# The gates of an encoder layer by Strassen's scheme, with their work placed among the attention heads

## The chip, the core and the metric

The kernel runs on one core of one Trainium2 chip. The core has TensorE (PE in the profile), which multiplies matrices out of the on-chip memory SBUF into the accumulator PSUM, VectorE (DVE), ScalarE (ACT) and GpSimd (POOL), which work on tensors elementwise, and queues that start DMA transfers: most are started by SyncE (SP), some by ACT. Each engine takes its own instructions in a fixed order and waits for the others by semaphores. The metric is the device time of one execution in microseconds (us); smaller is better.

## The reference

One residual layer over x, 1024 tokens by 1024 channels, all float32.

```python
h = rmsnorm(x, g_mix)
z = h @ w_in                     # 1024 x (512 pooling | 1024 q | 1024 k | 1024 v)
y_pool = pool_mixer(u_pool, w_pool_grp, pool_scale)
y_attn = diff_attention(q, k, v, ...)            # 8 heads, two softmax maps each
gates  = sigmoid(h @ w_gate + b_gate)            # 1024 x 2048
merged = gates[..., :D] * (y_pool @ w_branch_pool) + gates[..., D:] * (y_attn @ w_branch_attn)
x = x + merged @ w_out
h2 = rmsnorm(x, g_ffn)
x = x + square(relu(h2 @ w_up)) @ w_down         # 4096 hidden channels
```

The change is about one line of it, `h @ w_gate`: 1024 x 1024 by 1024 x 2048.

## The kernel before

**Arithmetic.** Each float32 operand is split into two parts, hi (rounded to the format that TensorE multiplies) and lo (the rest): ACT makes hi by a cast, DVE or POOL makes lo by a subtraction (`split`, lines 132 and 133). Each product of 128 x 128 weights with 128 x 512 inputs is then three matmuls, hi·hi, hi·lo and lo·hi (`mm3`, lines 153 to 155), accumulated in one PSUM bank of 128 x 512.

**Stages.** (1) x is normalised token block by token block, transposed on PE and split into `hT` (8 channel blocks by 2 token halves by hi and lo). (2) The heads: a loop over g = -2 to 71 with 64 steps of one head and 128 tokens each, software-pipelined. In one pass of the loop stand, for different steps, W (weights of the next head), A (the projection `z`, 24 matmuls of 384 columns), B (norms of q and k, with a power on POOL, tile `ms`), C (transposes `tk`; the result is cast to `Q`, and three DMAs from SP copy its parts to `K` and `Q`, lines 507 to 509), D (scores `sc` and softmax), E (transposes `ta`), F (`po`), H and R (norms of the result). (3) The branch projections: `bp` for the pooling branch, then `baX` and `baY` for the attention branch, where the gates multiply the results. (4) The output projection `op` for the 8 token blocks t, each followed by the second norm with transposes `hb` (`norm_token`). (5) The MLP up (`X`, `Y`, `Z`, `W`) and down (`Da`, `Db`). Stages 3 (attention branch) and 5 are already done by Strassen's scheme: of each 2 x 2 block product 7 block products are made in place of 8.

**Fillers.** The pooling projection (`u`, `yp`) and the gates (`g`, 16 column blocks of 128 by 2 token halves, 24 matmuls each) depend on `hT` alone. They are traced after the loop of the heads, and so have a lower priority than every step of it. A list scheduler sets the order of each engine's instructions when the kernel is built: it takes of what is ready in its own model of time what has the highest priority. So the fillers stand in the gaps of the heads' matmuls, in the order in which they were traced. `issue_after` and `queue_behind` add edges that only fix the order on one engine. The gates' first nine steps, with the loads of the attention weights `wq` that are started among them, are bound in this way behind the loads of x on SP. Banks: 2 for `z`, 1 for the fillers; the last gates may use the 2 banks of `z` too.

**After the gates.** A gate's result is copied from PSUM by ACT with its bias and stored to DRAM (`g_dram`); stage 3 loads it again and takes the sigmoid.

## Time and profile before

| what | value |
|---|---|
| time, median of 3 runs | 1529.0 us (1527.77 to 1530.09) |
| the profiled execution's own time | 1530.36 us |
| its span, first to last instruction | 1528.6 us |
| PE busy | 1515.5 us (99%), 7457 matmuls |
| DVE, ACT, POOL busy | 979.3, 757.6, 325.6 us |
| moved by DMA | 237.36 MB, mean 155 GB/s |

Busy time of PE is the union of the matmuls' durations. A matmul lasts from its start to its last result; the next one starts before that, so that durations overlap. The granted clock (PEclk) is a share of full speed. A page line of a group reads: line, engine, operation, output and inputs, shapes, count, busy time, mean duration in ns, then idle time of the engine before these instructions and who ended it.

### The profile page before, as it was taken

How to read it: one execution, taken by the hardware profiler on the slowest of the kernel's cores; microseconds unless marked ns; L12 is line 12 of the kernel's file. 1: busy time of each engine (PE TensorE's matmuls, PEld its weight loads, DVE VectorE, ACT ScalarE, POOL GpSimd, SP SyncE). 2: the span in 40 equal slices, each digit the busy share in tenths (PEclk: the TensorE clock that was granted, in tenths of full speed). 3: DMA queues.
4: the chain of work that ended last, by engine and by line, in shares of the span. 5: the costliest groups of instructions: out<-in, count | busy, mean ns of one | idle time of the engine just before them, and what ended most of it. 6: DMA issues, size and time to landing. Idle time of an engine off the chain costs nothing.

```text
span 1528.6 us, 21995 instructions
## 1 busy us (share of the span) xinstructions
PE 1515.5 (99%) x7457; PEld 1306.0 (85%) x7457; DVE 979.3 (64%) x2071; ACT 757.6 (50%) x1567; POOL 325.6 (21%) x413
## 2 busy tenths in 40 slices
PE   8999999999999999999999999999999999999999
PEld 6999999999999999888888887888888888888887
DVE  6666566667666666646578569666665668556572
ACT  6545455545454454454464456555555634333331
POOL 5677433334344342212100120000000000000000
PEclk9999999999999999999999999999999999999999
...
GB/s 233 125 167 166 105 63 87 68 82 89 68 92 77 90 131 70 248 89 240 133 213 208 226 117 148 153 181 152 142 134 111 268 326 403 172 124 262 227 193 28
DMA packets 195163, 237.36 MB, mean 155 GB/s; under 512 B 13974, under 2 KB 124523, under 8 KB 195052
## 3 DMA queue, kind: packets, MB, share of 16 engines
...
q8 instruction: 59, 0.97, 0.3%
q14 instruction: 52, 0.43, 0.1%
HBM read 157.24 MB, written 61.90 MB: 143 GB/s over the span
## 4 chain that ended last, share of the span: by engine, by line
PE 93%; DVE 2%; DMA 2%; ACT 1%; SPq 1%; issue 0%; ACTq 0%; DVEq 0%
PE z L153 6%; PE z L155 6%; PE z L154 6%; PE g L154 4%; PE g L155 4%; PE g L153 4%; PE Da L153 4%; PE Da L154 4%; PE Da L155 4%; PE Db L154 3%; PE Db L155 3%; PE Db L153 3%; PE X L153 2%; PE X L155 2%; PE X L154 2%; PE sc L535 2%
## 5 line engine op out<-in xcount | busy, mean ns | idle before, releaser
L153 PE MATMUL z<-wqkv,hT 128*128 128x384 f32 x512 | 176.6, 345 | 2.5 <-ACT hT L132 2.4
L154 PE MATMUL z<-wqkv,hT 128*128 128x384 f32 x512 | 175.6, 344 | 0.0
L155 PE MATMUL z<-wqkv,hT 128*128 128x384 f32 x512 | 174.8, 342 | 0.1
L546 ACT ACTIVATE s<-s,nm 128x256 f32<-128x256 f32 (+7 forms) x128 | 99.5, 778 | 62.2 <-DVE nm L538 61.4
L153 PEld LDWEIGHTS z<-wqkv,hT 128*128 128x128 f32 x512 | 97.6, 191 | 6.0 <-ACT hT L132 3.3
L153 PE MATMUL g<-hT,fwgate 128*128 128x512 f32 x256 | 100.6, 393 | 0.4 <-ACT hT L132 0.4
L155 PE MATMUL g<-hT,fwgate 128*128 128x512 f32 x256 | 101.0, 394 | 0.0
L154 PE MATMUL g<-hT,fwgate 128*128 128x512 f32 x256 | 100.9, 394 | 0.0
L155 PEld LDWEIGHTS z<-wqkv,hT 128*128 128x128 f32 x512 | 97.4, 190 | 2.8 <-DVE hT L133 0.6
L154 PEld LDWEIGHTS z<-wqkv,hT 128*128 128x128 f32 x512 | 97.6, 191 | 2.2
L477 POOL TENSOR_TENSOR ms<-ms,mhalf 128x4 f32<-128x4 f32 x64 | 69.2, 1081 | 138.3 <-DVE ms L476 137.8
L538 DVE CUSTOM_DVE_ANT_0 s<-sc,dist 128x512 f32<-128x512 f32 (+3 forms) x128 | 73.9, 584 | 38.4 <-PE sc L536 38.2
L133 DVE TENSOR_TENSOR AT<-ta,AT 128x256 fp32r<-128x256 f32 (+1 forms) x160 | 61.2, 392 | 47.8 <-ACT AT L132 47.4
L132 ACT CAST AT<-ta 128x256 fp32r<-128x256 f32 (+1 forms) x160 | 54.1, 349 | 50.0 <-PE ta L578 32.4
L133 DVE TENSOR_TENSOR AS<-s,AS 128x512 fp32r<-128x512 f32 x64 | 45.0, 704 | 37.7 <-ACT AS L132 37.6
L535 PE MATMUL sc<-K,Q 128*128 128x512 f32 (+2 forms) x192 | 68.1, 357 | 0.3 <-DMA Q<-Q 0.3
L536 PE MATMUL sc<-K,Q 128*128 128x512 f32 (+2 forms) x192 | 65.7, 347 | 0.0
L133 POOL TENSOR_TENSOR wqkv<-rqkv,wqkv 128x384 fp32r<-128x384 f32 x60 | 62.0, 1051 | 8.5 <-ACT wqkv L132 7.6
L133 POOL TENSOR_TENSOR fwgate<-frgate,fwgate 128x512 fp32r<-128x512 f32 x32 | 42.7, 1336 | 68.8 <-ACT fwgate L132 58.7
L153 PEld LDWEIGHTS g<-hT,fwgate 128*128 128x128 f32 x256 | 48.1, 188 | 8.9 <-ACT hT L132 0.7
L155 PEld LDWEIGHTS g<-hT,fwgate 128*128 128x128 f32 x256 | 48.1, 188 | 8.7
L154 PEld LDWEIGHTS g<-hT,fwgate 128*128 128x128 f32 x256 | 48.1, 188 | 8.5
(472 smaller groups left out, 4379.8 us busy)
## 6 DMA issues: line engine op xcount, KB each, us to landing
wd<-in_w_down_dram SPq DMA_DIRECT2D x56, 512.0 KB, 5.7
wu<-in_w_up_dram SPq DMA_DIRECT2D x32, 512.0 KB, 4.6
udS<-us SPq DMA_DIRECT2D x64, 256.0 KB, 2.1
ur<-udS SPq DMA_DIRECT2D x32, 512.0 KB, 3.4
...
ud<-u ACTq DMA_DIRECT2D x48, 256.0 KB, 3.0
ur<-ud SPq DMA_DIRECT2D x24, 512.0 KB, 7.3
frgate<-in_w_gate_dram SPq DMA_DIRECT2D x32, 256.0 KB, 2.7
```

What stands on the lines that cost most here:

```text
L132: a = nc.scalar.copy(hi, src)
L133: b = (lo_eng or nc.vector).tensor_tensor(lo, src, f(hi), op=ALU.subtract)
L153: nc.tensor.matmul(ps, lhs_hi, rhs_hi, start=first, stop=False, **kw)
L154: nc.tensor.matmul(ps, lhs_hi, rhs_lo, start=False, stop=False, **kw)
L155: return nc.tensor.matmul(ps, lhs_lo, rhs_hi, start=False, stop=last, **kw).ins
L477: nc.gpsimd.tensor_tensor(ms, ms, mhalf[:, 0:4], op=ALU.pow)
L535: nc.tensor.matmul(dst, Q[:, 1, i, :], rhs, start=True, stop=False)
L536: nc.tensor.matmul(dst, Q[:, 0, i, :], rhs, start=False, stop=True)
L538: nc.vector.tensor_tensor_reduce(out=s[i][:, c : c + w], in0=sc[:, 0:w], in1=dist[:, o0 + c : o0 + c + w], scale=2.0 ** -(h + 1), scalar=B ...
L546: nc.scalar.activation(s[i][:, 0:n], s[i][:, 0:n], AF.Exp, bias=last, scale=-1.0, accum_out=Z[:, i, t : t + 1])
```

## The change

**The product.** For each pair p of column blocks of `w_gate` (2p and 2p+1) the product with the two token halves is a 2 x 2 block product over two halves of the 1024 channels. It is made in 7 products of 4 x 3 matmuls, numbered as in `SIDES_G`. Weight sums S1 to S4 are made by POOL (`weight_sums`); three of them are stored to DRAM (`s_dram`) by DMAs that POOL itself starts, and come back when their product is due. The sums of the inputs, T1 to T4, are made once (`form`, at steps 12, 15, 18 and 21), split, stored in `t_dram` and loaded again (`place`): T1 and T3 into room of the fillers, T2 into room of the last head's weights, T4 over a quarter of `hT` that no product reads.

**The additions.** The parts of a result are added when a bank is emptied: DVE adds bank and part in one instruction (`plus`), and the part is stored again. The part comes from DRAM (`part`) into one of 3 buffers (`go`). Products 1 to 3 of all pairs run first, then the pooling groups among them, then all fifth products, then 6, 7 and 4 for pairs 0 to 2, 3 to 5 and 6 to 7, each triple in one bank that goes on accumulating (`last_products`).

**Where it runs.** The fillers are traced inside the loop of the heads (`fill_up(g)`), with priority numbers of their own that still lie behind all steps of the heads. Banks: 3, shared by `z` and the fillers. The edge that binds them behind the loads of x now covers the first step only.

**Other edits.** Buffers: `U` 11 to 10, `Q` 3 to 2, raw filler weights 2 to 4. In `weight_unit` hi and lo of the attention weights are made by ACT and DVE in place of POOL. The loads of the pooling result come before those of the attention result. In stage 4 `op7_0` is queued on PE behind the transposes `hb4` and `hb5`. All else is as before, at shifted lines (`mm3` is now 164 to 166, `split` 143 and 144).

```diff
-N_U, N_W, N_RAW, N_V = 11, 8, 2, 6
-N_FW, N_FR, N_FO = 4, 2, 2
-N_Q, N_QN = 3, 2
-N_Z, N_S, N_T, N_F = 2, 2, 2, 1
+N_U, N_W, N_RAW, N_V = 10, 8, 2, 6
+N_FW, N_FR, N_GO, N_FO = 4, 4, 3, 2
+N_Q, N_QN = 2, 2
+N_Z, N_S, N_T = 3, 2, 2
...
-PREP_AT = (2, 4, 6, 8)
+PREP_AT = (4, 7, 10, 12)
...
+ON_DVE = "5674"
+FILL = 3, 0.8
+FILLER = 1000000
+HB_FIRST = (4, 0), (5, 0)
+FORM_AT = 12, 15, 18, 21
...
-G_FIRST, G_Z = 9, 10
+G_FIRST = 12
...
-    g_dram = dram.tile([2 * D, S], F32, name="g_dram")
+    g_dram = dram.tile([NK, P, 4, 512], F32, name="g_dram")
+    t_dram = dram.tile([4, 4, P, 2, 512], F32, name="t_dram")
+    s_dram = dram.tile([NK, 3, P, 4, P], F32, name="s_dram")
...
+        def digits(rw, name, eng=nc.gpsimd):
+            w = fw_tile([P, 2, 4, P], name)
+            stored["lo"] = split(w[:, 0], w[:, 1], rw, eng).ins
+            return w
...
+        def side(name, k):
+            if name in QUARTERS:
+                kp, th = QUARTERS[name]
+                return tuple(hT[kp + k // 2, th, i][:, k % 2, :] for i in range(2))
+            return T[name][k]
+        def form(k):
+            def put(name, src):
+                t = fw_tile([P, 2, 512], f"T{name}_{k}")
+                split(t[:, 0, :], t[:, 1, :], src)
+                nc.sync.dma_start(t_dram["1234".index(name), k], f(t))
+            def sub_p(o, x_, y_):
+                nc.gpsimd.tensor_tensor(o, x_, y_, op=ALU.subtract)
+            def add_d(o, x_, y_):
+                nc.vector.tensor_tensor(o, x_, y_, op=ALU.add)
...
+            (b11, c11), (b12, c12), (b21, c21), (b22, c22) = (
+                tuple(f(i) for i in side(q, k)) for q in ("11", "12", "21", "22")
+            )
+            ta, tb = (fr_tile([P, 512], f"t{i}{k}") for i in "ab")
+            sub_p(ta, b22, b12)
+            sub_p(tb, c22, c12)
+            add_d(ta, ta, tb)
+            put("3", ta)
+            nc.gpsimd.tensor_tensor(tb, ta, b11, op=ALU.add)
+            add_d(tb, tb, c11)
+            put("2", tb)
+            tc_, td = (fr_tile([P, 512], f"t{i}{k}") for i in "cd")
+            sub_p(tc_, b21, tb)
+            add_d(tc_, tc_, c21)
+            put("4", tc_)
+            td2 = tb
+            sub_p(td, b12, b11)
+            sub_p(td2, c12, c11)
+            add_d(td, td, td2)
+            put("1", td)
+        def place(name):
+            for k in range(4):
+                if name == "T2":
+                    t = tuple(wt([P, 512], f"T{name}_{k}{i}") for i in "hl")
+                elif name in ("T1", "T3"):
+                    r = tpools[k // 2].tile([P, 2, 512], F32R, tag="T", name=f"T{name}_{k}")
+                    t = r[:, 0, :], r[:, 1, :]
+                else:
+                    t = tuple(hT[k // 2, 1, i][:, k % 2, :] for i in range(2))
+                for i in range(2):
+                    nc.sync.dma_start(f(t[i]), t_dram["1234".index(name[1]), k, :, i, :])
+                T.setdefault(name, []).append(t)
...
+        def side_w(p, name):
+            if name == "22":
+                return raw_block(p, name)
+            r = fr_tile([P, 4, P], f"fr{p}_{name}")
+            nc.sync.dma_start(r, s_dram[p, "S123".index(name[1]) - 1])
+            return r
...
+        def weight_sums(p):
+            a11, a12, a21, a22 = (raw_block(p, n) for n in ("11", "12", "21", "22"))
+            yield a11
+            yield a12
+            def made(i, o, x_, y_, op):
+                nc.gpsimd.tensor_tensor(o, x_, y_, op=op)
+                if i is not None:
+                    nc.gpsimd.dma_start(s_dram[p, i], o)
+            made(0, a22, a21, a22, ALU.add)
+            made(2, a21, a11, a21, ALU.subtract)
+            made(1, a11, a22, a11, ALU.subtract)
+            made(None, a12, a12, a11, ALU.subtract)
+            yield a12
+        def gate_product(p, j, ps, src=None, more=False):
+            a, b = SIDES_G[j]
+            r = src or side_w(p, a)
+            w = digits(r, f"fwg{p}_{a}", nc.vector if j in ON_DVE else nc.gpsimd)
+            for k in range(4):
+                hi, lo = side(b, k)
+                mm3(ps, w[:, 0, k, :], w[:, 1, k, :], hi, lo, not more and k == 0, k == 3, more)
+            return ps
+        def part(p, slot):
+            t = go_tile(f"gp{p}_{slot}")
+            nc.sync.dma_start(t, g_dram[p, :, slot, :])
+            return t
+        def plus(p, slot, ps, src, bias, dst=None):
+            dst = dst or src
+            if bias is None:
+                nc.vector.tensor_tensor(dst, ps, src, op=ALU.add)
+            else:
+                c = 2 * p + bias
+                nc.vector.scalar_tensor_tensor(dst, ps, cols[:, c : c + 1], src, op0=ALU.add, op1=ALU.add)
+            nc.sync.dma_start(g_dram[p, :, slot, :], dst)
+        def gates():
+            for p in range(NK):
+                for j, r in zip("123", weight_sums(p)):
+                    ps = gate_product(p, j, fill_bank(f"g{p}_{j}"), r)
+                    if j == "1":
+                        x1 = go_tile(f"gx{p}")
+                        nc.scalar.copy(x1, ps)
+                        nc.scalar.dma_start(g_dram[p, :, 2, :], x1)
+                    else:
+                        plus(p, int(j) - 2, ps, x1, 0, go_tile(f"go{p}_{j}"))
+                    yield
+        def fifth(p):
+            a, b = part(p, 1), part(p, 2)
+            ps = gate_product(p, "5", fill_bank(f"g{p}_5"))
+            plus(p, 1, ps, a, None)
+            plus(p, 3, ps, b, 1)
+        def last_products(pairs, between):
+            banks = {p: fill_bank(f"g{p}_") for p in pairs}
+            for n, (j, slot, bias) in enumerate((("6", 1, None), ("7", 3, None), ("4", 2, 1))):
+                for p in pairs:
+                    src = part(p, slot)
+                    plus(p, slot, gate_product(p, j, banks[p], None, n > 0), src, bias)
+                if between:
+                    between.pop(0)()
+        stored = {}
+        loaded = {}
...
+            def put(j, a):
+                d = buf[:, nput[0] % 2]
+                nput[0] += 1
+                nc.scalar.copy(d[:, 0, :].bitcast(F32R), a)
+                nc.vector.tensor_tensor(d[:, 1, :].bitcast(F32R), a, d[:, 0, :], op=ALU.subtract)
+                nc.sync.dma_start(digits[ORDER_BA.index((j, kk))][:, :, cs], d)
...
+        units_left = [(kk, ch) for kk in range(2) for ch in range(2)]
+        def gate_step():
+            more = next(gate_units, "end") != "end"
+            steps[0] += 1
+            if steps[0] in PREP_AT:
+                prepare_weights()
+            if steps[0] in FORM_AT:
+                form(form_steps.pop(0))
+            return more
...
+        def fillers():
+            with tc.issue_after(first_loads[-1]):
+                with tc.issue_after(marks["T22h"]):
+                    gate_step()
+                yield 1
+            for n in range(G_FIRST - 1):
+                gate_step()
+                yield 1
+            for g in range(4):
+                for _ in pool_group(g):
+                    yield 2
+                    gate_step()
+                    yield 1
+            while gate_step():
+                yield 1
+            assert not units_left and not form_steps
...
+            tpools.append(ts[0].enter_context(tc.tile_pool(name="ta", bufs=2, reuse_waits="tile")))
+            tpools.append(ts[1].enter_context(tc.tile_pool(name="tb", bufs=2, side="right", reuse_waits="tile")))
+            place("T1")
+            for p in range(NK):
+                fifth(p)
+                yield 1
+        fill = fillers()
+        at = [FILLER, 0]
+        def fill_up(g):
+            here, tc.cur_priority = tc.cur_priority, at[0]
+            while at[1] < (g - FILL[0]) * FILL[1]:
+                at[1] += next(fill, 1000)
+            at[0], tc.cur_priority = tc.cur_priority, here
         first_loads = list(x_loads)
...
+            fill_up(g)
...
+        tc.cur_priority = at[0]
+        for _ in fill:
+            pass
...
-    def gate_cols(c):
-        ws = fill_w(w_gate, c * P, f"gate{c}")
-        for th in range(2):
-            ps = fill_proj(ws, th, f"g{c}_{th}", spare_bank if c >= G_Z else fill_bank)
-            fo = fo_tile(f"go{c}_{th}")
-            nc.scalar.activation(fo[:, 0:512], ps, AF.Identity, bias=cols[:, c : c + 1])
-            nc.scalar.dma_start(g_dram[c * P : (c + 1) * P, th * 512 : (th + 1) * 512], fo[:, 0:512])
-            yield
-    def gates():
-        for c in range(2 * NK - 2):
-            yield from gate_cols(c)
-        for gen in [gate_cols(c) for c in (2 * NK - 2, 2 * NK - 1)] * 2:
-            next(gen)
-            yield
...
-            d = buf[:, nput[0] % 2]
-            nput[0] += 1
-            nc.gpsimd.tensor_copy(d[:, 0, :].bitcast(F32R), a)
-            nc.gpsimd.tensor_tensor(d[:, 1, :].bitcast(F32R), a, d[:, 0, :], op=ALU.subtract)
...
-    with tc.issue_after(first_loads[-1]):
-        with tc.issue_after(marks["T22h"]):
-            gate_step()
-        for _ in range(G_FIRST - 1):
-            gate_step()
-    for g in range(4):
-        for _ in pool_group(g):
-            gate_step()
-    while gate_step():
-        pass
...
+    place("T2")
+    forms = [lambda: place("T3"), lambda: place("T4")]
+    last_products((0, 1, 2), forms)
+    last_products((3, 4, 5), None)
+    last_products((6, 7), None)
...
+            gt, g_dram[r0 // 2, :, r0 % 2 * 2 + th, :]
...
+    for t, dh in HB_FIRST:
+        queue_behind(last[f"op{NT - 1}_{dh}"], last[f"hb{t}_1"])
```

**The order of the instructions.** First, SP's queue at the start of the program (`x1` to `x7` are blocks of 128 tokens, `rqkv` raw head weights, `frgate` or `fr0` raw gate weights, `wq` raw attention weights). Before:

```order
L333 DMA x1_167<-in_x_dram 128x1024
L333 DMA x2_219<-in_x_dram 128x1024
L333 DMA x3_233<-in_x_dram 128x1024
L384 DMA gqk_235<-in_g_q_dram 128x64
L386 DMA gqk_235<-in_g_k_dram 128x64
L389 DMA lqk_238<-in_lambda_qk_dram 128x256
L403 DMA rows_240<-in_b_gate_dram 16x128
L404 DMA rows_240<-in_pool_scale_dram 4x128
L405 DMA rows_240<-in_g_sub_dram 1x128
L333 DMA x4_283<-in_x_dram 128x1024
L333 DMA x5_285<-in_x_dram 128x1024
```

Now:

```order
L347 DMA x1_169<-in_x_dram 128x1024
L887 DMA wq0_0_981<-in_w_branch_attn_dram 128x2x256 x2
L347 DMA x2_221<-in_x_dram 128x1024
L347 DMA x3_235<-in_x_dram 128x1024
L398 DMA gqk_237<-in_g_q_dram 128x64
L400 DMA gqk_237<-in_g_k_dram 128x64
L403 DMA lqk_240<-in_lambda_qk_dram 128x256
L417 DMA rows_242<-in_b_gate_dram 16x128
L418 DMA rows_242<-in_pool_scale_dram 4x128
L419 DMA rows_242<-in_g_sub_dram 1x128
L347 DMA x4_286<-in_x_dram 128x1024
L347 DMA x5_288<-in_x_dram 128x1024
```

The two loads of `wq` stood behind the gates' raw weights, four rows behind `x5`; now they stand between `x1` and `x2`.

Second, SP's queue where the last head's tokens 2 and 3 are copied. Before:

```order
L507 DMA K7_0_5558<-Q7_2_5914 64x2x128
L508 DMA K7_0_5558<-Q7_2_5914 64x2x128
L509 DMA Q7_2_5914<-Q7_2_5914 64x512
L507 DMA K7_0_5558<-Q7_3_6004 64x2x128
L508 DMA K7_0_5558<-Q7_3_6004 64x2x128
L711 DMA frgate12_0_7842<-in_w_gate_dram 128x4x128
L509 DMA Q7_3_6004<-Q7_3_6004 64x512
L507 DMA K7_1_5559<-Q7_4_6072 64x2x128
L711 DMA frgate12_1_7847<-in_w_gate_dram 128x4x128
L508 DMA K7_1_5559<-Q7_4_6072 64x2x128
L509 DMA Q7_4_6072<-Q7_4_6072 64x512
```

Now:

```order
L521 DMA K7_0_6899<-Q7_2_7333 64x2x128
L522 DMA K7_0_6899<-Q7_2_7333 64x2x128
L787 DMA hT0_1_0_342<-t_dram_135 128x512
L521 DMA K7_0_6899<-Q7_3_7449 64x2x128
L523 DMA Q7_2_7333<-Q7_2_7333 64x512
L522 DMA K7_0_6899<-Q7_3_7449 64x2x128
L787 DMA TT2_0h_7974<-t_dram_135 128x512
L787 DMA TT2_0l_7975<-t_dram_135 128x512
L523 DMA Q7_3_7449<-Q7_3_7449 64x512
L787 DMA TT2_1h_7978<-t_dram_135 128x512
L787 DMA TT2_1l_7979<-t_dram_135 128x512
L521 DMA K7_1_6900<-Q7_4_7543 64x2x128
```

Between the copies of `Q7_2` and `Q7_3` now stand loads of T4 (into `hT0_1_0`) and of T2. The load into `hT0_1_0` has to wait until the last projection `z7_7` has read that tile; the first product 6 on PE reads `TT2_0h`.

Third, PE at the last transposes `hb7` of stage 4 (`X1`, `Y1` are products of the MLP's second pair, `X2` of its third). Before:

```order
L155 MATMUL X1_10159<-B11h_9212,A11_1_10161 128x512
L153 MATMUL X1_10159<-B11h_9212,A11_1_10161 128x512
L1162 MATMUL hb7_0_10099<-identf_96,y7_9835 128x128 x4
L154 MATMUL X1_10159<-B11l_9213,A11_1_10161 128x512
L155 MATMUL X1_10159<-B11h_9212,A11_1_10161 128x512
L153 MATMUL X1_10159<-B11h_9212,A11_1_10161 128x512
L1162 MATMUL hb7_1_10100<-identf_96,y7_9835 128x128 x4
L154 MATMUL X1_10159<-B11l_9213,A11_1_10161 128x512
```

Now:

```order
L165 MATMUL Y1_10586<-B21l_9642,A12_1_10604 128x512
L166 MATMUL Y1_10586<-B21h_9641,A12_1_10604 128x512
L1342 MATMUL hb7_0_10525<-identf_102,y7_10262 128x128 x4
L164 MATMUL Y1_10586<-B21h_9641,A12_1_10604 128x512
L165 MATMUL Y1_10586<-B21l_9642,A12_1_10604 128x512
L166 MATMUL Y1_10586<-B21h_9641,A12_1_10604 128x512
L164 MATMUL X2_10652<-B11h_9639,A11_2_10654 128x512
L165 MATMUL X2_10652<-B11l_9640,A11_2_10654 128x512
L1342 MATMUL hb7_1_10526<-identf_102,y7_10262 128x128 x4
L166 MATMUL X2_10652<-B11h_9639,A11_2_10654 128x512
```

After the transposes `hb6`, 31 matmuls of products stood ahead of `hb7_0` (`X0` 12, `Y0` 12, `X1` 7); now it is 45 (`X0`, `Y0`, `X1` 12 each, `Y1` 9), and the output projection that ends last is `op7_0` in place of `op7_1`.

270 lines of the change are left out of this document (139 added, 131 removed).

## The prediction

> **What bounds the kernel now.** I read the page first, for which engine never rests; then the windows, for what a matmul costs in each stage; then the timeline, to see whether matmuls truly follow each other.
>
> ```profile
> span 1528.6 us, 21995 instructions
> PE 1515.5 (99%) x7457; PEld 1306.0 (85%) x7457; DVE 979.3 (64%) x2071; ACT 757.6 (50%) x1567; POOL 325.6 (21%) x413
> PE 93%; DVE 2%; DMA 2%; ACT 1%; SPq 1%; issue 0%; ACTq 0%; DVEq 0%
> ...
> L153 PE MATMUL g<-hT,fwgate 128*128 128x512 f32 x256 | 100.6, 393 | 0.4 <-ACT hT L132 0.4
> ...
> 500.00:600.00 100.00, 100.00 (x568) 91.62 (x567) 65.09 (x210) 52.53 (x144) 34.00 (x40) 1.00 0.32 96
> ...
> 900.00:950.00 50.00, 47.09 (x217) 38.20 (x216) 47.67 (x74) 34.35 (x64) 10.02 (x8) 1.00 0.37 116
> ...
> 1100.00:1200.00 100.00, 100.00 (x443) 82.82 (x442) 61.38 (x95) 57.34 (x100) 0.00 (x0) 1.00 0.40 141
> ```
>
> In a window the columns are stretch, then busy us and count of PE, PEld, DVE, ACT and POOL, then granted clock, DMA share and GB/s. PE is busy in all of its span but 13 us, and 93% of the chain that ended last is PE. The gates' group says 393 ns for one matmul, but that is from its start to its last result: in the window from 1100 to 1200 us, where all matmuls have 512 columns, 443 of them fill 100 us, or 0.226 us each. The timeline shows the same among the heads:
>
> ```profile
> 302.08 0.39 PE L153 MATMUL g<-hT,fwgate 128*128 128x512 f32 x1
> 302.31 0.40 PE L154 MATMUL g<-hT,fwgate 128*128 128x512 f32 x1
> 302.55 0.40 PE L155 MATMUL g<-hT,fwgate 128*128 128x512 f32 x1
> ```
>
> Each lasts 0.39 to 0.40 us, and the next starts 0.23 to 0.24 us later. So the currency is starts on PE: a matmul that goes away gives back 0.226 to 0.235 us, as long as the next one is ready.
>
> **Matmuls removed.** The gates had 16 blocks x 2 halves x 24 = 768; now they have 8 pairs x 7 products x 12 = 672. All else on PE stays in number. 96 x 0.226 = 21.7 us (96 x 0.224 to 96 x 0.235: 21.5 to 22.6). They stand among the heads, where the window from 500 to 600 us has PE at 100.00 of 100, so I count all of it: **-21.7**.
>
> **The start.** In the new order of SP two loads of `wq` come between the blocks x1 and x2.
>
> ```profile
> 6.58 1.46 SPq L333 DMA_DIRECT2D x<-in_x_dram  x3
> 14.68 1.54 SPq L333 DMA_DIRECT2D x<-in_x_dram  x2
> 21.87 1.36 SPq L807 DMA_DIRECT2D wq<-in_w_branch_attn_dram  x2
> ...
> 14.75 1.06 ACT L280 ACTIVATE hn<-x 128x1024 f32<-128x1024 f32 x1 [0.15 <-DMA x<-in_x_dram]
> ...
> 24.78 1.37 ACT L132 CAST fwgate<-frgate 128x512 fp32r<-128x512 f32 x2 [3.05 <-DMA frgate<-in_w_gate_dram]
> ...
> 27.43 0.45 PE L153 MATMUL z<-wqkv,hT 128*128 128x384 f32 x1 [1.58 <-ACT hT L132]
> ...
> 8.00:16.00 8.00, 7.19 (x25) 6.53 (x24) 5.17 (x10) 6.95 (x17) 5.40 (x5) 1.00 0.83 283
> 16.00:25.00 9.00, 8.85 (x54) 7.87 (x53) 8.45 (x24) 4.77 (x14) 5.08 (x8) 1.00 0.94 282
> 25.00:29.00 4.00, 2.06 (x14) 1.42 (x13) 1.80 (x7) 3.86 (x10) 3.52 (x5) 1.00 0.94 340
> 29.00:33.00 4.00, 4.00 (x18) 3.91 (x16) 3.24 (x10) 3.43 (x9) 2.71 (x4) 0.57 0.43 131
> ```
>
> Here DMA is the limit: ACT waits for x2 (0.15 us, so no slack), and then 3.05 us for the raw gate weights, with the casts of `hT` behind it; PE waits 1.58 us for those. The two loads are 2 x 256 KB = 0.52 MB, at 282 GB/s 1.9 us. x2, x3 and all that is queued behind them land that much later, the gate weights too, and PE waits 3.5 us in place of 1.58. Behind the gate weights the queue has caught up, since `wq` is no longer there. **+1.9**; nothing if the later loads give it back, and up to 3.6 if the slow stretch behind the wait (granted clock 0.57 from 29 to 33 us, 4 x 0.43 = 1.7 us) comes a second time.
>
> [...]
>
> **The last head's end.** While the last head runs, the sums T2 (8 loads of 256 KB) must come into the room of its weights, and SP waits at T4's first load for the last projection to begin.
>
> ```profile
> K<-Q SPq DMA_DIRECT2D x128, 64.0 KB, 2.0
> Q<-Q SPq DMA_DIRECT2D x64, 128.0 KB, 2.2
> g<-g_dram SPq DMA_DIRECT2D x32, 256.0 KB, 3.7
> g_dram<-go ACTq DMA_DIRECT2D x32, 256.0 KB, 2.4
> ur<-ud SPq DMA_DIRECT2D x24, 512.0 KB, 7.3
> ...
> L507 SPq DMA_DIRECT2D K<-Q x64: 590/597/858, 47.0 to 641.9; - x64
> L509 SPq DMA_DIRECT2D Q<-Q x64: 472/485/553, 51.2 to 644.7; - x64
> ...
> 307.12 0.38 PE L498 MATMUL tk<-identf,qn 128*128 128x128 f32 x2
> ```
>
> Count from the first matmul of that projection. On PE 24 projections' matmuls (4.2 us at the 0.174 of the projections' own starts) and some 12 small ones come before the first product 6: 5.5 us. On SP come a load (0.32), two copies to K (0.6 each), the first T2 load (0.32) and its landing (3.7): 5.5 us too. Its last load must be there when PE has done 6.7 us more, 12.2 after the start; 2.6 MB at 282 GB/s take 9.2 us, with 0.3 + 1.2 + some 0.5 before it 11.2. Both are about even, with nothing to spare. I take **+1.5**; nothing at best, and 4 if the first landing takes 7.3 us like the 512 KB loads of `ur`. Behind a matmul that waits here stand the last head's own scores.
>
> **The output projection.** With 45 in place of 31 matmuls between `hb6` and `hb7_0`, PE comes there 14 x 0.226 = 3.2 us later.
>
> ```profile
> 907.75 1.53 POOL L1146 TENSOR_TENSOR y<-y,gfb 128x512 f32<-128x512 f32 x1 [6.78 <-DMA yd<-y]
> 916.37 4.33 POOL L1159 TENSOR_SCALAR y<-y,nrs 128x512 f32<-128x512 f32 x2
> ...
> 918.45 0.66 PE L1162 MATMUL hb<-identf,y 128*128 128x128 f32 x4 [1.00 <-POOL y L1159]
> 920.76 0.66 PE L1162 MATMUL hb<-identf,y 128*128 128x128 f32 x4 [0.97 <-POOL y L1159]
> 947.32 0.50 PE L153 MATMUL X<-BT3h,AS 128*128 128x512 f32 x1 [0.94 <-ACT U L1325]
> ```
>
> That covers the waits of 1.00 and 0.97. But POOL's first multiplication (1.53 us) works on the half that `op7_0` makes; that half now ends last, and the multiplication joins the chain: 3.2 - 1.5 = 1.7 against 1.97. And DVE, at 47.67 of 50 us from 900 to 950, is late next. **-1.0**; at best all three waits go (-2.9), at worst DVE takes the gain and 1 us more.
>
> **Parts of the gates.** A product of 6, 7 or 4 needs its part loaded (3.7), added and stored (2.4) through one of three buffers. The addition is DVE's, from a bank; an addition of that shape:
>
> ```profile
> L237 DVE TENSOR_TENSOR mp<-bp,g x16: 674/680/692, 700.0 to 740.9; 128x512 f32<-128x512 f32 x16
> ```
>
> A buffer's turn is 3.7 + 0.7 + 2.4 = 6.8 us; three products take PE 36 x 0.226 = 8.1. So it costs nothing, covered by 1.3 us of PE's own work; what the cover is worth is a rival below.
>
> **Among the heads.** The elementwise work grows. DVE gets 56 additions of parts (38 us by the row above), and hi or lo parts and sums, some 60 us of it within the first 550: 65 of 100 us busy become 76. POOL loses half of its splits and gets 56 sums of 128 x 512 at the price of
>
> ```profile
> L133 POOL TENSOR_TENSOR fwgate<-frgate,fwgate 128x512 fp32r<-128x512 f32 x32 | 42.7, 1336 | 68.8 <-ACT fwgate L132 58.7
> L477 POOL TENSOR_TENSOR ms<-ms,mhalf 128x4 f32<-128x4 f32 x64 | 69.2, 1081 | 138.3 <-DVE ms L476 137.8
> ```
>
> 75 us; it stays under half busy. Neither becomes a bound, but `ms`, on each step's way to its scores, more often finds a sum of 1.3 us ahead. From `tk` to the scores PE has at the tightest step 5.9 us of other matmuls (7.6 before). The chain across: a cast and subtraction (0.4 each, with the hand-overs 1.9 together), K 0.6, K 0.6, Q 0.49, landing 2.2: 5.8. So the tightest steps have nothing to spare. With one buffer less of `Q` and of `U`: **+1.0**, from nothing to 8 (an eighth of a microsecond in each of 64 steps).
>
> **Sum.** The profiled execution took 1530.4 us by its own time (1528.6 its span, 1.8 around it), 1.4 above the median. 1530.4 - 21.7 + 1.9 + 1.5 - 1.0 + 1.0 = 1512.1; against the median **1511 us**. All bounds at their best give 1529.0 - 22.6 - 2.9 = 1503.5; all at their worst 1529.0 - 21.5 + 3.6 + 4 + 1 + 8 = 1524.
>
> **Rivals.**
> *The parts set the pace* at the end. Both transfers would have to take as long as the longest 256 KB ones:
>
> ```profile
> U2y<-yd SPq DMA_DIRECT2D x4, 256.0 KB, 5.9
> out_dram<-z5y SPq DMA_DIRECT2D x4, 256.0 KB, 4.9
> ```
>
> Then a turn is 5.9 + 0.7 + 4.9 = 11.5 us, 3.8 per product in place of 2.7. Over the 16 products that stand closely that is 18 us: 1511 + 18 = 1529, no change. It decides once a turn takes over 8.1 us. For it: T2, T4, the parts and the weights' sums bring more than 250 GB/s into that stretch, against a mean of 155. Against it: a product may be late by the work of two others before its bank is wanted again.
>
> *SP stands still.* The raw weights of the next pair reuse buffers that still hold sums until the stores that POOL starts have landed; SP waits for that in front of `K<-Q` and `Q<-Q`. No run here shows a DMA started by POOL. By the nearest rows such a store takes a POOL instruction of 1.3 us and a landing of up to 3.2:
>
> ```profile
> wa_dram<-wd SPq DMA_DIRECT2D x28, 256.0 KB, 3.2
> ```
>
> 4.5 us, where the usual step has 7.6 - 5.8 = 1.8 to spare: 2.7 for each exposed one. All 24 make 65 us, 1511 + 65 = 1576; from the eighth on the gain is gone (8 x 2.7 = 22), with ten the time is 1538. This is the slower side. For it: the order has up to seven other transfers between the copies of one step, before at most four. Against it: SP mostly stands waiting for `Q` anyway:
>
> ```profile
> SPq L507 <- ACT Q L504: 107.1, 27, 8.7
> ```
>
> [...]
>
> *The durations are the price.* If PE really gave back 393 ns for each matmul, the sum would start from 96 x 0.393 = 37.7, and the time be 1495. The starts 0.23 us apart speak against it.
>
> **How the numbers follow.** Forecast 0.78, parts 0.10, SP 0.08, durations 0.04. The range of 1504 to 1525 is the forecast's own by its bounds, and leaves out the others. What a measurement of this kernel can tell from no change is about 0.2%, 3 us: faster means below 1526. Faster: the forecast, the durations and half of the parts' case, 0.87. Same: the other half, 0.05. Slower: 0.08.
>
> **What would show it.** Right: PE near 99% of a span of about 1510; 672 starts for `g`, still 0.23 us apart; x2 waited for some 2 us longer by ACT at the start; no PE wait above 2 us from 60 us on. Wrong: PE idle in front of `g` behind `T2` or `part` (the first rival), in front of `sc` behind `Q<-Q` in the first 300 us (the second), or a span under 1500 (the third).

## The result, and the profile after

The changed kernel takes **1604.3 us** (median of 4 runs, 1600.7 to 1607.1), the kernel before 1529.6 beside it: a ratio of 1.0485, 95% interval 1.0455 to 1.0514. Forecast were 1511 us, with a range of 1504 to 1525. The change is 75 us slower, and the forecast missed by 93.

The page of the changed kernel, with the lines that answer to those shown of before (span, busy time, chain):

```profile
span 1598.7 us, 22332 instructions
PE 1525.3 (95%) x7361; PEld 1296.3 (81%) x7361; DVE 1099.9 (69%) x2223; ACT 770.9 (48%) x1611; POOL 375.0 (23%) x425
PE 71%; DMA 10%; DVE 10%; ACT 3%; issue 3%; POOL 2%; SPq 1%; POOLq 0%; DVEq 0%; ACTq 0%
```

The 96 matmuls are gone (7457 to 7361), but the chain that ended last is now only 71% PE, where it was 93%. The windows show where. First before, then after; columns as in the prediction.

```profile
50.00:150.00 100.00, 99.74 (x563) 91.85 (x563) 64.29 (x200) 50.94 (x143) 74.22 (x106) 1.00 0.54 165
150.00:550.00 400.00, 400.00 (x2251) 366.74 (x2250) 259.42 (x827) 207.16 (x559) 159.36 (x189) 1.00 0.30 86
550.00:800.00 250.00, 250.00 (x1218) 213.18 (x1217) 152.77 (x348) 122.86 (x258) 49.34 (x40) 1.00 0.49 160
```

```profile
50.00:150.00 100.00, 85.13 (x439) 72.93 (x438) 79.48 (x185) 45.51 (x130) 67.81 (x71) 0.97 0.62 189
150.00:550.00 400.00, 377.16 (x2072) 338.69 (x2073) 298.98 (x837) 205.14 (x554) 208.75 (x226) 0.99 0.44 128
550.00:800.00 250.00, 230.59 (x1148) 197.22 (x1147) 169.20 (x435) 108.18 (x259) 46.97 (x47) 0.98 0.75 238
1100.00:1200.00 100.00, 100.00 (x443) 82.81 (x442) 63.51 (x100) 56.04 (x99) 0.00 (x0) 1.00 0.43 144
```

From 1100 to 1200 us PE starts 443 matmuls in both kernels. Nearly everything is lost in the first 800 us, and not at one place: PE misses 15 of 100 us, then 23 of 400, then 19 of 250. DVE and the DMA queues are busier in all three stretches, POOL only from 150 to 550 us.

Busy time hides part of it, because a late matmul also overlaps less with the next. So I also added up, from the starts of all matmuls, by how much each comes later than its undisturbed spacing (0.2265 us behind a matmul of 512 columns, 0.173 behind 384, 0.115 behind 256, 0.109 behind 128). I call this PE's **lateness**. It holds waits and slower clock together.

| lateness of PE, us | 0–50 | 50–150 | 150–550 | 550–800 | from 800 | sum |
|---|---|---|---|---|---|---|
| before | 13.8 | 2.0 | 5.8 | 2.1 | 5.3 | 29.0 |
| changed | 17.0 | 24.4 | 39.2 | 31.2 | 10.0 | 121.8 |

The difference is 92.8 us; less the 21.7 of the matmuls it is 71.1, against a span longer by 70.1. The account closes: what is left to explain is late starts, by waits or by a slower clock.

### The profile page after: what moved, and what is told of

Same layout as the page of the kernel before. It is cut to its first block, busy times and chain, and to the rows that moved or that the text cites. A ratio compares the mean times of both kernels' runs of the same rounds, so it can differ in the third digit from the quotient of the medians.

```text
span 1598.7 us, 22332 instructions
## 1 busy us (share of the span) xinstructions
PE 1525.3 (95%) x7361; PEld 1296.3 (81%) x7361; DVE 1099.9 (69%) x2223; ACT 770.9 (48%) x1611; POOL 375.0 (23%) x425
## 4 chain that ended last, share of the span: by engine, by line
PE 71%; DMA 10%; DVE 10%; ACT 3%; issue 3%; POOL 2%; SPq 1%; POOLq 0%; DVEq 0%; ACTq 0%
PE Da L165 4%; PE Da L164 4%; PE Da L166 4%; PE Db L165 3%; PE Db L166 3%; PE Db L164 3%; PE z L164 3%; PE X L166 3%; PE X L164 3%; PE X L165 3%; PE z L165 2%; PE z L166 2%; PE Z L165 2%; PE Z L166 2%; PE Z L164 2%
## 5 line engine op out<-in xcount | busy, mean ns | idle before, releaser
L491 POOL TENSOR_TENSOR ms<-ms,mhalf 128x4 f32<-128x4 f32 x64 | 71.1, 1111 | 127.2 <-DVE ms L490 126.9
L549 PE MATMUL sc<-K,Q 128*128 128x512 f32 (+2 forms) x192 | 71.0, 371 | 24.1 <-DMA Q<-Q 13.7
L143 ACT CAST AT<-ta 128x256 fp32r<-128x256 f32 (+1 forms) x160 | 53.5, 350 | 44.7 <-PE ta L592 21.8
L144 DVE TENSOR_TENSOR AT<-ta,AT 128x256 fp32r<-128x256 f32 (+1 forms) x160 | 60.2, 389 | 14.1 <-ACT AT L143 13.8
L144 DVE TENSOR_TENSOR AS<-s,AS 128x512 fp32r<-128x512 f32 x64 | 43.7, 686 | 36.0 <-ACT AS L143 35.8
L144 POOL TENSOR_TENSOR wqkv<-rqkv,wqkv 128x384 fp32r<-128x384 f32 x60 | 63.8, 1085 | 14.0 <-ACT wqkv L143 14.0
L550 PE MATMUL sc<-K,Q 128*128 128x512 f32 (+2 forms) x192 | 66.2, 350 | 0.0
L549 PEld LDWEIGHTS sc<-K,Q 128*128 128x128 f32 x192 | 36.6, 190 | 34.4 <-issue 8.5
L500 POOL TENSOR_TENSOR qn<-qn,ggh 128x128 f32<-128x128 f32 x64 | 34.1, 534 | 101.4 <-DVE qn L494 77.3
L614 PE MATMUL po<-AT,V 128*128 128x512 f32 x128 | 50.1, 410 | 2.4 <-DVE AT L144 2.3
L164 PE MATMUL op<-wo,mT 128*128 128x512 f32 x128 | 50.8, 397 | 0.0
L165 PE MATMUL op<-wo,mT 128*128 128x512 f32 x128 | 50.5, 396 | 0.0
L166 PE MATMUL op<-wo,mT 128*128 128x512 f32 x128 | 50.5, 396 | 0.0
L592 PE MATMUL ta<-identf,s 128*128 128x128 f32 x288 | 44.8, 273 | 4.6 <-DVE s L569 2.9
```

The costliest lines, as they stand in the source:

```text
L143: a = nc.scalar.copy(hi, src)
L144: b = (lo_eng or nc.vector).tensor_tensor(lo, src, f(hi), op=ALU.subtract)
L164: nc.tensor.matmul(ps, lhs_hi, rhs_hi, start=first, stop=False, **kw)
L165: nc.tensor.matmul(ps, lhs_hi, rhs_lo, start=False, stop=False, **kw)
L166: return nc.tensor.matmul(ps, lhs_lo, rhs_hi, start=False, stop=last, **kw).ins
L491: nc.gpsimd.tensor_tensor(ms, ms, mhalf[:, 0:4], op=ALU.pow)
```

## The experiments

All were timed in 3 rounds (e14 in 5) against the kernel before on the same chip. Ratios are those to before, with their 95% intervals; the changed kernel's is 1.0485 (1.0455 to 1.0514). It was not timed again beside the experiments, so two kernels are compared by their ratios, and a difference of some 0.3% between two of them, 5 us, is not clear of noise.

### One suspect at a time

**e1** puts the attention weights' hi and lo, and the last of the sums ahead of them, back on POOL; **e2** does only that part of the change to the kernel before (the same edit, reversed).

```diff
-nc.scalar.copy(d[:, 0, :].bitcast(F32R), a)
-nc.vector.tensor_tensor(d[:, 1, :].bitcast(F32R), a, d[:, 0, :], op=ALU.subtract)
+nc.gpsimd.tensor_copy(d[:, 0, :].bitcast(F32R), a)
+nc.gpsimd.tensor_tensor(d[:, 1, :].bitcast(F32R), a, d[:, 0, :], op=ALU.subtract)
```

> The changed kernel, with hi and lo of the attention weights (`wd`) made by POOL again, as before. Theory 'blocked port': the loss comes from DVE instructions with two inputs in SBUF, which stand still while POOL computes (58 us of stretched DVE instructions between 50 and 550 us, against 18 before). Then this brings little, since POOL gets its copies and subtractions back: 1596 to 1612 us. Theory 'wait in line': ACT stands at the stores of `wd` (14 waits, 18 us) with the heads' casts behind it; then the stretch from 50 to 150 us loses its 24 us of PE's idle time nearly down to the 2 us of before: 1580 to 1586 us.

> The kernel before, with only this one part of the change: hi and lo of the attention weights made by ACT and DVE in place of POOL. Theory 'wait in line': ACT stands at the stores here too, 1543 to 1550 us (15 to 20 more). Theory 'blocked port': without POOL's new sums nothing is blocked for long, 1527 to 1535 us.

e1: 1598.1 us, 1.0465 (1.0449 to 1.0481). e2: 1539.5 us, 1.0074 (1.0058 to 1.0090). e2 lies between its two ranges, e1 in that of 'blocked port', though barely faster than the changed kernel. Alone the part costs 11 us, nearly all of it between 50 and 150 us (lateness 12.5 in place of 2.0). The timeline of ACT in the changed kernel shows how:

```profile
54.60 0.37 ACT L518 CAST Q<-tk 128x256 fp32r<-128x256 f32 x1 [1.78 <-PE tk L512]
56.37 0.41 ACT L896 CAST wd<-wq 128x256 fp32r<-128x256 f32 x1 [1.40 <-DMA wa_dram<-wd]
59.02 0.41 ACT L896 CAST wd<-wq 128x256 fp32r<-128x256 f32 x1 [2.24 <-POOL wq L901]
61.59 0.41 ACT L896 CAST wd<-wq 128x256 fp32r<-128x256 f32 x1 [2.17 <-DMA wa_dram<-wd]
63.71 0.41 ACT L896 CAST wd<-wq 128x256 fp32r<-128x256 f32 x1 [1.72 <-DMA wa_dram<-wd]
64.03 0.37 ACT L518 CAST Q<-tk 128x256 fp32r<-128x256 f32 x1
```

From 55 to 64 us ACT makes four casts of 0.4 us and otherwise stands in front of them, mostly until the store of the tile has landed. The heads' next cast to `Q` stands behind. Before, POOL waited here. In e2 too ACT stands at these casts, for 15.7 us between 40 and 160 us, and DVE, which has their subtractions too, is busy for 66.0 us from 50 to 150 us (64.3 before, 79.5 in the changed kernel), so there it is the waiting and not 'blocked port'. Yet undoing it in the changed kernel (e1) brought less than that: 50 to 150 us became 8 us better, and PE then lost 8.5 of 50 us at 200 us (3.5 in the changed kernel).

```profile
200.00:250.00 50.00, 41.53 (x212) 35.20 (x211) 36.99 (x122) 25.36 (x72) 23.68 (x35) 0.90 0.43 121
```

**e3** moves all 56 sums, in `weight_sums` and `form`, from POOL to DVE (the first diff shows one of the three places; POOL still starts the stores), **e4** traces the loads of `ypT` behind those of the attention result again.

```diff
-nc.gpsimd.tensor_tensor(o, x_, y_, op=op)
+nc.vector.tensor_tensor(o, x_, y_, op=op)
```

```diff
-ypT = [load_split(p_dram, g * P, f"ypT{g}", ypt_tile) for g in range(4)]
 for d in range(NK - 2):
     yr[d] = y_scaled(d, row_factors(d))
+ypT = [load_split(p_dram, g * P, f"ypT{g}", ypt_tile) for g in range(4)]
```

> The changed kernel, with the 56 sums of weights and inputs that POOL makes (128 x 512, 1.3 us each there) made by DVE (0.7 us each). 'Blocked port': POOL's work beside DVE is 75 us less, most of the stretched DVE instructions go, and PE's idle time from 50 to 550 us falls by 20 to 45 us: 1560 to 1585 us. If instead DVE's own load sets the pace among the heads, its 38 us more make it slower: 1606 to 1625 us.

> The changed kernel, with the loads of the pooling result `ypT` traced behind those of the attention result again, as before. Now ACT waits 10 us for three of these loads between 618 and 640 us, with the last head's casts behind it. If that sets the pace there, the 7.6 us that PE loses from 600 to 650 us go: 1594 to 1599 us. If the parts of the gates on SP set it, 1601 to 1607 us.

e3: 1606.7 us, 1.0524 (1.0506 to 1.0541). e4: 1603.7 us, 1.0497 (1.0469 to 1.0526). Neither helps; e3 is in the range of 'DVE's own load', e4 in that of 'the parts'. e3 was meant for something that the timeline of the changed kernel shows on DVE and POOL:

```profile
78.57 0.62 POOL L817 DMA_DIRECT2D s_dram<-fr  x1
78.71 0.42 DVE L494 TENSOR_TENSOR qn<-z,ms 128x256 f32<-128x256 f32 x1
79.05 3.69 DVE L897 TENSOR_TENSOR wd<-wq,wd 128x256 fp32r<-128x256 f32 x1
79.21 1.31 POOL L815 TENSOR_TENSOR fr<-fr,fr 128x512 f32<-128x512 f32 x1
80.46 1.98 POOL L144 TENSOR_TENSOR wqkv<-rqkv,wqkv 128x384 fp32r<-128x384 f32 x2
82.39 0.65 POOL L500 TENSOR_TENSOR qn<-qn,ggh 128x128 f32<-128x128 f32 x1
```

A DVE subtraction of 128 x 256 with both inputs in SBUF lasts 3.69 us, where the median of the 28 of its line is 0.45, beside three POOL instructions that follow each other (the row of L144 holds two). DVE started at 79.05, before POOL's 79.21, and ended at 82.74, after the third of them (82.44). Counting by how much DVE's instructions exceed the lower quartile of their own line and shape (0.1 us or more), they lasted 58 us longer between 50 and 550 us in the changed kernel, 18 before, and 32 in e3. In the changed kernel these are 65 instructions, and each of them overlaps one of POOL's. Of the 58 us 16 are the attention weights' subtractions (L897), so two edits of the change collide here. Moving the sums freed 26 us of it, but put 38 us of new work on DVE (56 x 0.68), and POOL then stood 20.7 us at the stores of sums that DVE had not yet made; the time stayed. In these traces DVE is held up beside POOL's work, by 58 us in the changed kernel; what this costs by itself is not shown.

**e6** takes the banks apart (2 for `z`, 1 for the fillers), **e7** gives `Q` its third buffer back, **e8** takes the buffers of `Q` and `U` from the kernel before, **e10** traces all fillers behind the loop again, with the banks of e6. In this order, e6 in `fill_bank` and e10 in the loop of the heads:

```diff
-        return ps_z.tile([P, 512], F32, tag="z", name=name)
+        return ps_f.tile([P, 512], F32, tag="f", name=name)
...
-N_Q, N_QN = 2, 2
+N_Q, N_QN = 3, 2
...
-N_U, N_W, N_RAW, N_V = 11, 8, 2, 6
-N_Q, N_QN = 3, 2
+N_U, N_W, N_RAW, N_V = 10, 8, 2, 6
+N_Q, N_QN = 2, 2
...
-        fill_up(g)
```

> The changed kernel with banks apart as before: 2 for z, 1 for the fillers, and the last products in all 3. If the sharing of banks makes the heads late (a projection waits for a filler's bank until DVE or ACT has emptied it): 1570 to 1592 us. If not: 1600 to 1615 us, no faster, since a filler product of 2.7 us now has a single bank.

> The changed kernel with 3 buffers of Q in place of 2. If the buffer is what makes the scores late (a Q is cast only after the scores of two steps ago): PE's 14 us of waits for the copy to Q fall by half and all that follows with them, 1575 to 1595 us. If DVE's and ACT's queues are the cause: 1598 to 1608 us.

> The kernel before with 2 buffers of Q in place of 3 and 10 of U in place of 11. If these buffers alone cost the heads their slack: 1540 to 1560 us. If not: 1526 to 1532 us.

> The changed kernel with all its fillers traced behind the loop of the heads, as before, and banks apart (2 for z, 1 for the fillers). If the place among the heads is the cause: 1520 to 1560 us. If it is Strassen's own transfers and elementwise work: 1590 to 1620 us.

e6: 1601.6 us, 1.0491 (1.0465 to 1.0517). e7: 1608.5, 1.0527 (1.0511 to 1.0543). e8: 1531.4, 1.0018 (1.0008 to 1.0027). e10: 1602.9, 1.0492 (1.0477 to 1.0508). e6, e8 and e10 are in the range that acquits what they test; e7 is just above its own, so a third `Q` does not help. Banks, buffers and the place where the fillers are traced are not the cause by themselves; the buffers cost 3 us.

### The scheme itself

**e5** was to show whether the elementwise work or the structure is at fault, and left out nearly all the work: the weight sums, the arithmetic of `form` (quarters of `hT` are stored in its place), and loads and additions of parts; the attention weights as in e1.

```diff
-nc.gpsimd.tensor_tensor(o, x_, y_, op=op)
...
+nc.sync.dma_start(t_dram[i, k, :, 0, :], hi)
+nc.sync.dma_start(t_dram[i, k, :, 1, :], lo)
...
-nc.sync.dma_start(t, g_dram[p, :, slot, :])
...
-nc.vector.tensor_tensor(dst, ps, src, op=ALU.add)
+nc.scalar.copy(dst, ps)
```

> The changed kernel with only its matmuls, banks, buffers and order left. Left out: the arithmetic of POOL's weight sums (raw weights are stored in their place), the whole forming of T1 to T4 (parts of the input are stored in their place), the loads of the parts of the gates and their additions (ACT copies each bank with its bias and SP stores it); and the attention weights' hi and lo are on POOL again. Theory 'elementwise load' (so much more work on DVE, ACT, POOL and SP among the heads that each step comes late): PE's waits go back to about 0.8 us in 50, and the time to 1508 to 1530 us. Theory 'structure' (the shared banks, the buffers or the place of the fillers among the heads): most of the waits stay, 1560 to 1600 us.

1576.5 us, 1.0326 (1.0309 to 1.0343): by its own terms for "structure". But it was badly made. It kept all the stores, and since nothing has to be computed for `t_dram` any more, 16 of its 32 were started in the first 50 us, which moved 310 GB/s in that window (186 before). It is not used further.

**e9** turns the question round: the new structure with plain gates, 24 matmuls to a bank that ACT empties, and without `form`, `place`, `fifth` and `last_products`.

```diff
-for p in range(NK):
-    for j, r in zip("123", weight_sums(p)):
...
+for c in range(2 * NK):
+    ws = fill_w(w_gate, c * P, f"gate{c}")
+    for th in range(2):
+        ps = fill_proj(ws, th, f"g{c}_{th}")
```

> The changed kernel with the plain gates of before (16 column blocks by 2 halves, 24 matmuls each, ACT empties the bank, no sums, no parts) in the new place: traced among the heads' steps, on the 3 shared banks, with the other buffers and the attention weights' hi and lo on ACT and DVE. 96 more matmuls than the changed kernel, 21.7 us. If the place and the shared banks cost the heads their slack, the waits stay: 1565 to 1600 us. If Strassen's scheme itself does (its many small transfers, loads and additions per matmul): 1530 to 1548 us, of which some 12 are the attention weights.

1570.7 us, 1.0281 (1.0264 to 1.0298). By the time alone this is the first of the two expectations, but the windows say otherwise:

```profile
150.00:550.00 400.00, 398.79 (x2205) 361.48 (x2204) 256.01 (x795) 205.89 (x546) 159.76 (x184) 1.00 0.33 91
550.00:700.00 150.00, 150.00 (x815) 135.18 (x814) 77.67 (x248) 67.58 (x177) 43.09 (x48) 1.00 0.37 111
700.00:750.00 50.00, 31.47 (x118) 23.81 (x117) 33.12 (x78) 23.62 (x50) 9.71 (x7) 0.78 0.48 155
```

From 150 to 700 us PE runs nearly as full as before (lateness 7.1 in 150–550, 5.8 before). Some 29 us are lost in one piece behind 700 us, where the fillers are used up and the last head's steps stand alone: a fault of this experiment, which holds no gates back for the end. So in the stretch where the changed kernel loses 33 us, its place among the heads, its shared banks and its buffers do no harm to plain gates. Strassen's own work does.

**e11**, **e12** and **e13** leave out its two kinds of work, apart and together; **e15** and **e16** split the first. The diff shows in turn the weight sums S (left out in e11, e13, e16), T (e11, e13, e15) and the parts (e12, e13):

```diff
-made(0, a22, a21, a22, ALU.add)
...
+for n in ("11", "12", "21"):
+    yield raw_block(p, n)
...
-FORM_AT = 12, 15, 18, 21
+FORM_AT = ()
...
-"5": ("S1", "T1"),
-"6": ("S2", "T2"), "7": ("S3", "T3"), "4": ("22", "T4"),
+"5": ("S1", "12"),
+"6": ("S2", "21"), "7": ("S3", "22"), "4": ("22", "11"),
...
-nc.sync.dma_start(t, g_dram[p, :, slot, :])
...
-nc.vector.tensor_tensor(dst, ps, src, op=ALU.add)
+nc.scalar.copy(dst, ps)
```

> The changed kernel without Strassen's sums. Left out: POOL's sums of weights, their stores and reloads (each product loads a raw block of weights instead, three per pair at first and four later), and T1 to T4 altogether (the products take quarters of the input itself). The parts of the gates, with their loads and DVE's additions, stay. If the sums (POOL's 75 us, DVE's 50 us of T, 13 MB stored and loaded) cost the heads their slack: 1555 to 1580 us, and PE's waits from 200 to 550 us near 5 us in place of 34. If the parts do: 1590 to 1605 us.

> The changed kernel without the parts. Left out: the loads of the parts of the gates and their additions; ACT copies each bank with its bias and SP stores the copy. Sums and T1 to T4 stay. If the parts set the pace from 550 us on (the chain there holds 19 us of their stores and loads): 1575 to 1590 us. If sums do it there too, nothing comes of it: 1595 to 1606 us.

> The changed kernel with neither sums nor parts (both of the above left out): 672 matmuls for the gates in products of 12, each with its own load and split of weights and its own copy out of the bank. If sums and parts are the whole cause, what is left is the attention weights' preparation (12) and the start (3): 1508 - 1509 matmuls' own, so 1515 to 1530 us. If products as small as 12 matmuls are a cause of their own: 1545 to 1575 us.

> The changed kernel without T1 to T4 (left out: their forming, stores and loads; the products take quarters of the input itself). POOL's weight sums with their stores and reloads, and the parts, stay. Leaving out both kinds of sums brought 33 us. If T brings most of that: 1570 to 1582 us. If the weight sums do: 1592 to 1602 us.

> The changed kernel without POOL's weight sums (left out: the sums and their stores; raw blocks are loaded in their place). T1 to T4 and the parts stay. If the weight sums and POOL's stores bring most of the 33 us: 1570 to 1582 us. If T does: 1592 to 1602 us.

| kernel | time, us | ratio to before | lateness 50–150 | 150–550 | 550–800 |
|---|---|---|---|---|---|
| changed | 1604.3 | 1.0485 (1.0455 to 1.0514) | 24.4 | 39.2 | 31.2 |
| e11, no sums | 1570.6 | 1.0283 (1.0261 to 1.0306) | 14.0 | 18.0 | 36.8 |
| e12, no parts | 1599.8 | 1.0466 (1.0444 to 1.0487) | 24.2 | 54.9 | 21.8 |
| e13, neither | 1543.4 | 1.0106 (1.0092 to 1.0121) | 9.4 | 19.4 | 15.2 |
| e15, no T | 1590.0 | 1.0412 (1.0395 to 1.0428) | 27.0 | 19.8 | 39.8 |
| e16, no S | 1584.1 | 1.0379 (1.0358 to 1.0400) | 16.5 | 26.3 | 34.2 |

In place of the sums raw blocks are loaded; in place of the additions ACT copies the bank. Of the expectations, e11 met the range of 'the sums', with more lateness left than it said, e12 that of 'nothing comes of it', and e13, e15 and e16 fell between their two ranges.

This settles the larger part. Together sums and parts cost 3.8% of 1527, 58 us. They share it: without the sums the parts cost 27 us (e11 against e13), with them 3, which is less than the intervals (e12 against changed). That 3 is a balance: 9 us better from 550 to 800 us, 16 worse from 150 to 550, and SP still stands 80 us at the stores of ACT's copies, where it stood 91 at the parts' loads and stores. So e12 trades one wait for another, and does not price the parts. The sums cost 31 us with the parts and 55 without. Of the sums T costs 11 and S 16 us, which nearly add up to 31. What is left in e13 is 16 us above before although 21.7 us of matmuls are gone: 38 us, of which e2 sizes 11. The rest, which goes with products of 12 matmuls (56 splits of weights and 64 copies out of a bank, in place of 32 of each), is not taken apart.

**e17** and **e18** ask whether the sheer load is enough: 48 useless subtractions on POOL (as in the diff), or on DVE (`nc.vector`), in the kernel before.

```diff
 ws = fill_w(w_gate, c * P, f"gate{c}")
+r0, r1 = raws2[-2:]
+for o, x_, y_ in ((r1, r0, r1), (r0, r0, r1), (r1, r0, r1)):
+    nc.gpsimd.tensor_tensor(o, x_, y_, op=ALU.subtract)
```

> The kernel before with 48 useless subtractions of 128 x 512 on POOL, three per block of gate columns on its raw weights, behind their split; no transfers and nothing that waits for them but the raw buffer. 48 x 1.3 = 64 us of POOL. If POOL's instructions by themselves hold up DVE (both read two tiles of SBUF) or the power of the heads' norms: 1537 to 1560 us. If only what hangs on the sums counts (transfers, later weights): 1526 to 1532 us.

> The same 48 subtractions in the kernel before, on DVE: 48 x 0.7 = 33 us. If DVE's load by itself costs the heads their slack: 1535 to 1560 us. If 73 of 100 us busy in place of 65 do no harm: 1526 to 1532 us.

e17: 1534.4 us, 1.0044 (1.0028 to 1.0060), between its two ranges. e18: 1531.7, 1.0027 (1.0017 to 1.0036). The windows from 150 to 550 us, of e17 and then of e18:

```profile
150.00:550.00 400.00, 400.00 (x2273) 368.84 (x2272) 271.45 (x859) 210.88 (x574) 176.42 (x208) 1.00 0.30 85
```

```profile
150.00:550.00 400.00, 398.59 (x2244) 365.61 (x2243) 269.53 (x849) 210.13 (x566) 154.22 (x185) 1.00 0.30 84
```

17 us more of POOL, or 10 of DVE, cost PE next to nothing there. Work that nobody waited for was cheap here: 64 us on POOL cost 7 in the end, 33 on DVE cost 4. But the test is milder than the change, which brought 49 us of POOL and 40 of DVE into the same stretch. That the sums hurt because products and transfers hang on them, and not by their load, is thus made likely and not shown.

**e14** does the edit of the output projection alone to the kernel before (`queue_behind(op7_0, hb4)` and `hb5`).

> The kernel before with the one edit of the output projection alone: op7_0 queued on PE behind the transposes hb4 and hb5. Prediction: 1.0 us faster (0 to 2.9). The changed kernel waits 6.9 us there from 950 to 1050 us, where before waited 3.8; if that is this edit's doing, 2 to 4 us slower.

1527.9 us, 1.0006 (0.9997 to 1.0015): no difference that can be measured. No kernel of the study beats the kernel before.

## Why the prediction was wrong, point by point

**Matmuls removed: right.** All 96 are gone, and undisturbed ones still start 0.226 us apart. That all of it comes off the time because PE is at 100.00 of 100 there was the error of reasoning behind the rest: it held only as long as PE stayed the bound.

**The start: right in kind, +3.2 in place of +1.9.** The waits that were to grow did, for the gate weights and the casts behind them above all.

```profile
14.98 1.06 ACT L296 ACTIVATE hn<-x 128x1024 f32<-128x1024 f32 x1 [1.20 <-DMA x<-in_x_dram]
25.13 1.38 ACT L143 CAST fwg<-fr 128x512 fp32r<-128x512 f32 x2 [4.33 <-DMA fr<-in_w_gate_dram]
27.78 0.69 PE L164 MATMUL z<-wqkv,hT 128*128 128x384 f32 x1 [2.99 <-ACT hT L143]
```

ACT waits 4.33 us in place of 3.05, PE 2.99 in place of 1.58 (forecast 3.5). Of x2 it is less: ACT waits 1.20 us in place of 0.15, but starts on it only 0.23 us later than before. The upper case of 3.6 nearly came true: the clock was at half for 6.8 us from 26.9 us on (0.52 from 27 to 34 us), where it was for 3.4 before. That is 1.7 us more, beside 1.4 of longer wait.

**Among the heads, +1.0 with an upper end of 8: this is the step that failed.** Between 50 and 550 us the lateness grew by 56 us. I counted the busy time of DVE and POOL, found both below 80% and 50%, and concluded "Neither becomes a bound". In the row of DVE the forecast was even good (76 of 100; it is 299 of 400, part of it standing still). But an engine that works in a fixed order doesn't need to be full to be late. The tightest steps had 5.9 us of cover against a chain of 5.8, as I had worked out myself, and I let 64 such steps pay an eighth of a microsecond each. And I never priced the waits of one edit, the attention weights on ACT and DVE: 11 us by e2.

That check of the cover was itself short in two ways. Its chain left out a wait that the kernel before has already: SP starts the copy to `Q` only when the copies to `K` have landed, 1.3 us on average (us in all, times, longest).

```profile
SPq L509 <- DMA K<-Q: 88.8, 68, 3.9
```

And it looked at one crossing only, from `tk` to the scores. PE's longest waits in the changed kernel from 30 to 800 us:

```profile
PE sc L549 <- DMA Q<-Q: 13.7, 9, 3.9
PE po L635 <- ACT oqs L143: 8.0, 4, 4.2
PE sc L549 <- DVE nm L552: 4.7, 7, 1.0
PE z L164 <- DVE gp L846: 3.8, 2, 3.2
PE ta L592 <- DVE s L569: 2.9, 3, 1.2
```

Of 57 us in all (0.3 before), 24 stand in front of the scores. The other 33 stand in front of `po`, `z`, `ta` and the fillers, for which the prediction had no cover worked out.

In the chain of waits from 150 to 550 us, 400 of 400 us are PE in before. In the changed kernel, added up by engine, 234 are PE, 70 DVE, 37 DMA, 24 ACT, 21 issue, 11 POOL. Its row of shares by line:

```profile
by line: PE z L164 8.1%; PE z L166 7.9%; PE z L165 7.9%; issue 5.1%; PE u L164 4.0%; PE u L165 3.6%; PE u L166 3.5%; PE po L614 3.0%; PE g L164 3.0%; DVE s L552 2.8%; DMA rqkv<-in_w_in_dram 2.8%; PE sc L549 2.8%; PE g L165 2.7%; PE g L166 2
```

Outside PE and "issue" no line has more than 3% (12 us). That agrees with the experiments, where no single repair helped clearly and only leaving work out did.

**Parts of the gates, 0: wrong by the rival's own condition.** I took a turn of 6.8 us and named 8.1 as the point from which it decides. From 550 to 800 us the issues read (last column: us to landing), and SP's waits over the whole run:

```profile
g_dram<-gp SPq DMA_DIRECT2D x40, 256.0 KB, 4.1
gp<-g_dram SPq DMA_DIRECT2D x37, 256.0 KB, 4.3
```

```profile
SPq L836 <- DMA g_dram<-gp: 45.8, 26, 3.8
...
SPq L797 <- DMA s_dram<-fr: 11.9, 2, 8.4
```

4.3 + 0.7 + 4.1 = 9.1 us. The landings of the kernel before (3.7 and 2.4) do not hold in a stretch that moves 238 GB/s in place of 160, and the rival had itself reckoned with such a rate. SP stood 45.8 us in front of the parts' loads, and while the heads ran their copies were queued behind. e11 against e13 gives 27 us for the parts without the sums.

**The last head's end, +1.5: right place, too small.** There a copy to `K` took 5.50 us to land (64 KB; 2.0 before), between loads of T3 and T4, and PE waited for the copy to `Q` behind it. Chain, then timeline:

```profile
655.10 5.50 DMA K<-Q
660.62 2.26 DMA Q<-Q
662.97 0.41 PE sc L549
```

```profile
662.97 0.41 PE L549 MATMUL sc<-K,Q 128*128 128x384 f32 x1 [2.46 <-DMA Q<-Q]
...
665.05 0.19 PEld L164 LDWEIGHTS g__7990<-TT_0h,fwg_S 128*128 128x128 f32 x1 [1.47 <-DMA TT_0h<-t_dram]
```

Then the first product 6 waited for T2, as forecast: its weights 1.47 us, PE itself 1.15. Behind both waits the clock was at half for 3.4 us (0.50 from 665.2 to 668.6 us), 1.7 us more: 5.3 us in all, where at worst 4 were forecast.

**The output projection, −1.0: right where it was aimed, outweighed beside it.** The two waits for POOL in front of `hb7`, 1.00 and 0.97 us before, shrank:

```profile
993.56 0.66 PE L1342 MATMUL hb<-identf,y 128*128 128x128 f32 x4 [0.18 <-POOL y L1339]
995.95 0.66 PE L1342 MATMUL hb<-identf,y 128*128 128x128 f32 x4 [0.58 <-POOL y L1339]
```

The wait of 0.94 behind them became 0.27, so that the three fell by 1.9 us. But from 800 us on the lateness is 4.7 us more, and the largest piece stands two tokens earlier:

```profile
974.20 1.44 PE L1342 MATMUL hb<-identf,y 128*128 128x128 f32 x8 [2.50 <-ACT y L1414]
```

These transposes wait 2.50 us for ACT's copy out of an earlier `hb` bank, which had itself waited 3.29 us for DVE; behind it the clock was at half for 3.4 us (0.51 from 975.8 to 979.2 us). The kernel before has no such wait. Nor has e14, where the edit alone left the three waits as they were (1.09, 0.97 and 1.07 us). So it is not this edit by itself; whether the edit takes part in it is not shown.

**The rivals.** "Slower" had a chance of 0.08 and one mechanism, SP standing still behind POOL's stores. The side was right, the mechanism hardly: the row of `s_dram` above has two such waits, 11.9 us in all, and the stores that POOL started landed after 3.1 us (median of 12) up to 150 us and 2.4 from there on. That the time came out on its side was not its doing. "The parts set the pace" was right as a mechanism and too small. What no case held is what happened: many delays of a few tenths of a microsecond to 4 us, on every engine, that no longer fitted under the cover.
